# A hybrid S5/HGRN2 decoder block: the first ScalarE reader of each loaded tile tied into program order, and loads, squares, GELU and GLU operands in stages

## The chip, the cores and the metric

The kernel runs on one core of a Trainium2 chip. The metric is device microseconds of one execution, the median of several runs; a profiled execution of the same program gives the trace.

## The reference

x is 2048 tokens of 1024 channels, all float32. One block is computed:

```python
xn = rms_norm(x, norm_w)
proj = xn @ w_in            # 1024 x 5632
u_a, z_a, q_b, f_b, i_b, og_b, z_b, g_a, g_b = split(proj)
y_a = s5_branch(u_a, z_a, ...)    # 32 groups, 64-dim complex diagonal scan, GELU, GLU, * silu(z_a)
y_b = hgrn2_branch(q_b, f_b, i_b, og_b, z_b, ...)   # 4 heads of 128, chunked gated recurrence
merged = sigmoid(g_a) * (y_a @ w_proj_a) + sigmoid(g_b) * (y_b @ w_proj_b)
return rms_norm(x + merged @ w_out, final_norm_w)
```

## The kernel before

**Precision.** A float32 operand of a large product is split into two float32r parts: ScalarE copies it (`hi`), VectorE subtracts (`lo`). This is `split` (L118 to L120), so nearly every such copy has line L119 and every subtraction L120. Each product is three matmuls (hi*hi, hi*lo, lo*hi).

**Stages.** The tokens are two halves, a = 0 and 1. The input projection is done per slice of 256 columns by a seven-product Strassen scheme (`strassen`, L425 on): per product p there are twelve 128x512 matmuls, and PSUM is copied out by L464 (`u`, `s`, ScalarE) and L467 (VectorE). d0 and d1 are the projections of the two halves. Between their products, and in the tail after d1, other work is laid in by hand: HGRN2 (`hgrn_core`, `hgrn_fin`), the state-space branch (`ssm_build`, then `ssm_batch` for eight batches per half), `gelu`, the GLU (`glu_prep` prepares its operands, `glu` multiplies), `merge`, and the output projection (`out_w` loads and splits its weights, `out_proj` multiplies).

**Order.** TensorE's order is written out: `timed` (L1372) steps a generator of dense work, one step of mostly twelve matmuls at a time, and ahead of step t runs the events due at t. An event steps another generator to its next `yield`. The other engines' queues are filled by the framework's scheduler: it goes by program order as priority, but issues an instruction earlier when it takes its inputs to be there, by its own estimate of when loads land. Each queue is then executed in order, so an instruction whose tile has not landed holds everything behind it. All loads and most stores are issued on SP's queue; `u_evac`, `gate_evac` and `ssm_batch` store through ScalarE's.

**Tiles.** Pools have few buffers: `y` tiles (128x1024) two, `wr` tiles (128x1024) three, `wo` five, `s` five, `e` two, `r` (128x512) 56. A tile of a pool is given out again when its last reader is through; a load into it waits for that on SP's queue.

**What the change touches.** `norm_stats` (L178) squares x of one quarter for the RMS norm; for a = 1 it is called at steps 2 and 8 of d0's run with HGRN2, each time four loads into `y` tiles and four squares with accumulation (L189 to L191). `x_load` (L285) reloads transformed x (`xq`, in a `y` tile) and splits it (`X1..h`). `stage_w` and `split_w` (L306 to L320) load and split a projection weight. `w_ops` (L370) loads a raw input weight (`rw`, `get`, L381) and forms the seven Strassen operands; for a = 0 these are stored to DRAM (`wc`, L391) and for a = 1 reloaded (L375). `ssm_batch` (L748) loads W/U and V/M (each pair one tile: WU from `y` or `wr`, VM from `wr` or `wo`), builds or reloads cos/sin (CC, SS; `csv` stores them for the other half, L782), then does the products `psg` (L791), the rotation and scan, and `psy` (L829), whose result goes to `y_d`. `gelu` (L837) reloads `y_d` into a `y` tile `yy`, copies it reordered into the `wr` tile `ya` (L844), and needs a square, two VectorE operations, a sigmoid and a product before `ya` is stored (L851). `glu_prep` (L1171) loads `ya` in pairs into `y` tiles (`gy`) and z (`gz`), splits (`gh`, `gl`) and multiplies z. `glu` (L1188) takes one step per output tile: matmuls, sigmoid `gs`, product, split into `yh`, `yl`.

## Time and profile before

| | us |
|---|---|
| median of three runs | 1539.39 (1536.45 to 1541.62) |
| the profiled execution | 1540.05 |
| its span, first to last instruction | 1538.3 |
| TensorE busy in it | 1467.0 |
| VectorE busy | 1100.8 |
| ScalarE busy | 637.6 |
| TensorE's mean granted clock | 0.984 of full speed |

Busy time counts an instruction's own time, waits of the next instruction on the same engine are its idle time, and the trace names what ended each such wait. PE is TensorE, DVE VectorE, ACT ScalarE, SP the queue of SyncE. A line name can be a helper's (L119 is every ScalarE split), so tiles tell groups apart. Times of the rows below are microseconds from the span's start unless marked ns.

### The profile page before, as it was taken

The numbers are of one execution on the slowest core, as the hardware profiler recorded it, in microseconds if no ns is written. First come the engines' busy times: TensorE is split into PE (matmuls) and PEld (weight loads), VectorE is DVE, ScalarE is ACT, GpSimd is POOL, SyncE is SP. The second block draws the span as 40 slices with busy tenths as digits, with TensorE's granted clock in tenths as the row PEclk, the third lists the DMA queues.
The fourth block names the chain that finished last, engine by engine and source line by source line (L and its number), as shares of the span: only waits on it lengthen the run. The fifth ranks groups of instructions, "written<-read, shape, count | busy, mean of one in ns | idle before, by whom it ended". The sixth has DMA issues, their size and how long they took to land.

```text
span 1538.3 us, 21386 instructions
## 1 busy us (share of the span) xinstructions
PE 1467.0 (95%) x7360; PEld 1207.3 (78%) x7360; DVE 1100.8 (72%) x2409; ACT 637.6 (41%) x1391; POOL 3.6 (0%) x24
## 2 busy tenths in 40 slices
PE   7997999999999999999989999999989899899997
PEld 5776788788888777878878887788878688688886
DVE  5798688678678659956665887776649877765445
ACT  7456454454454634323323455333353332532222
POOL 0000000000000000000000000000000000000000
PEclk9998999999999999999999999999999999999999
DMA  9539778977977883786668559677977854854602
GB/s 336 175 115 305 284 278 295 316 255 269 331 264 286 285 271 119 186 245 197 231 201 313 174 163 294 217 259 264 327 236 234 266 184 137 274 171 131 212 14 103
DMA packets 192060, 354.53 MB, mean 230 GB/s; under 512 B 65680, under 2 KB 74896, under 8 KB 191952
## 3 DMA queue, kind: packets, MB, share of 16 engines
q1 hardware_dynamic: 163792, 328.00, 63.6%
q10 hardware_dynamic: 28160, 25.17, 4.8%
q8 instruction: 58, 0.95, 0.3%
q14 instruction: 50, 0.41, 0.1%
HBM read 214.17 MB, written 138.94 MB: 230 GB/s over the span
## 4 chain that ended last, share of the span: by engine, by line
PE 68%; DVE 15%; DMA 10%; ACT 3%; issue 3%; SPq 0%; ACTq 0%; DVEq 0%
PE pd L458 14%; PE pd L460 13%; PE pd L459 13%; PE pf L1284 3%; PE pf L1285 3%; PE pf L1286 3%; PE pp L1112 2%; PE pp L1111 2%; PE pp L1110 2%; PE sc L979 2%; DMA y_d<-T 1%; DVE w L120 1%; DMA xb<-in_xt_dram 1%; DMA xq<-xo_d 1%; PE pd L355 1%
## 5 line engine op out<-in xcount | busy, mean ns | idle before, releaser
L119 ACT ACTIVATE w<-rw 128x512 fp32r<-128x512 f32 x110 | 68.7, 628 | 112.7 <-PE pd L460 67.9
L1284 PE MATMUL pf<-ho,mh 128*128 128x512 f32 x256 | 101.2, 395 | 5.2 <-ACT mh L119 5.2
L1286 PE MATMUL pf<-ho,ml 128*128 128x512 f32 x256 | 100.6, 393 | 0.5 <-DVE ml L120 0.5
L1285 PE MATMUL pf<-lo,mh 128*128 128x512 f32 x256 | 100.3, 392 | 0.0
L464 ACT ACTIVATE u<-pd 128x512 f32<-128x512 f32 x80 | 47.5, 594 | 106.0 <-PE pd L460 103.3
L120 DVE TENSOR_TENSOR w<-rw,w 128x512 fp32r<-128x512 f32 x110 | 75.3, 685 | 16.9 <-ACT w L119 16.6
L467 DVE TENSOR_TENSOR u<-u,pd 128x512 f32<-128x512 f32 x80 | 54.8, 685 | 33.5 <-PE pd L460 22.8
L355 PE MATMUL pd<-xh,hw 128*128 128x512 f32 x128 | 52.4, 409 | 9.0 <-ACT hw L119 6.7
L1284 PEld LDWEIGHTS pf<-ho,mh 128*128 128x128 f32 x256 | 48.6, 190 | 15.4 <-ACT mh L119 5.5
L1286 PEld LDWEIGHTS pf<-ho,ml 128*128 128x128 f32 x256 | 48.4, 189 | 11.6 <-DVE ml L120 1.6
L1285 PEld LDWEIGHTS pf<-lo,mh 128*128 128x128 f32 x256 | 48.6, 190 | 9.9
L119 ACT ACTIVATE mh<-sgl 128x512 fp32r<-128x512 f32 x32 | 20.0, 629 | 86.7 <-DVE sgl L1227 86.3
L356 PE MATMUL pd<-xl,hw 128*128 128x512 f32 x128 | 51.2, 400 | 0.0
L357 PE MATMUL pd<-xh,lw 128*128 128x512 f32 x128 | 50.9, 397 | 0.0
L980 DVE COPY_PREDICATED s_buf<-masks,sc 128x256 f32<-128x256 uint8 x64 | 32.5, 508 | 25.0 <-PE sc L979 25.0
L1110 PE MATMUL pp<-yh,hpa 128*128 128x512 f32 x128 | 50.2, 392 | 0.0
L1112 PE MATMUL pp<-yh,lpa 128*128 128x512 f32 x128 | 49.9, 390 | 0.2 <-DVE lpa L120 0.2
L1111 PE MATMUL pp<-yl,hpa 128*128 128x512 f32 x128 | 50.0, 390 | 0.0
L1226 DVE TENSOR_TENSOR sgl<-sgl,pp 128x512 f32<-128x512 f32 x48 | 32.7, 683 | 23.0 <-PE pp L1112 22.9
L1016 DVE TENSOR_TENSOR Q<-Q,t 128x256 f32<-128x256 f32 x96 | 40.5, 422 | 10.0 <-PE sc L991 9.9
L974 ACT ACTIVATE KX<-K 128x128 f32<-128x128 f32 x128 | 32.6, 304 | 35.6 <-DVE K L1017 26.3
L979 PEld LDWEIGHTS sc<-Q,KX 128*128 128x128 f32 x256 | 38.0, 189 | 8.9 <-issue 1.8
(915 smaller groups left out, 4431.6 us busy)
## 6 DMA issues: line engine op xcount, KB each, us to landing
wc<-w SPq DMA_DIRECT2D x126, 512.0 KB, 3.4
w<-wc SPq DMA_DIRECT2D x126, 512.0 KB, 4.6
rw<-in_wi_dram SPq DMA_DIRECT2D x44, 512.0 KB, 4.6
sgl<-sg_d SPq DMA_DIRECT2D x48, 256.0 KB, 3.2
sg_d<-u ACTq DMA_DIRECT2D x32, 256.0 KB, 3.5
ro<-in_wo_dram SPq DMA_DIRECT2D x16, 512.0 KB, 5.1
hh<-in_xn_dram SPq DMA_DIRECT2D x32, 256.0 KB, 5.1
out_dram<-hh SPq DMA_DIRECT2D x32, 256.0 KB, 2.4
```

The lines of the kernel that those rows point to most:

```text
L119: S.activation(hi, raw, AF.Copy)
L120: V.tensor_tensor(lo, raw, hi.bitcast(F32), op=ALU.subtract)
L458: mm(o, w[:, 0, k], xh, start=(first and k == 0), stop=False, skip_group_check=True)
L459: mm(o, w[:, 0, k], xl, start=False, stop=False, skip_group_check=True)
L460: mm(o, w[:, 1, k], xh, start=False, stop=(k == 3), skip_group_check=True)
L979: mm(ps[:, :, c, :], ch(kx, c), qp, start=True, stop=True)
L1110: mm(ps, hi[:, k, fs], yh, start=(k == 0), stop=False)
L1111: mm(ps, hi[:, k, fs], yl, start=False, stop=False)
L1112: mm(ps, lo[:, k, fs], yh, start=False, stop=(k == last))
L1284: mm(o, mh[:, ts_], hi, start=(kk == 0), stop=False)
L1285: mm(o, mh[:, ts_], lo, start=False, stop=False)
L1286: mm(o, ml[:, ts_], hi, start=False, stop=(kk == 7))
```

## The change

`pin(ins)` ties an instruction behind the one that the program has just before it on the same engine, so that the scheduler can't issue it earlier; it adds an order, not a wait for a result. `split` gets `hold`, which pins its ScalarE copy; it is set where the copied tile was just loaded: `x_load`, `split_w`, `yb_load`, `glu_w`, `glu_prep`, `out_w`. `norm_stats` keeps only a = 0; for a = 1 `norm_stats1` loads two tiles ahead and squares over ten steps, pinned. `gelu` becomes five stages with the first of its four copies pinned; `glu_prep` loads both pairs in two steps and splits in four more; `glu_w` and `out_w` yield between load and split; `ssm_batch` loads E first, then W/U, then V/M, and stores cos/sin after the rotation; the steps of the events are moved to match. In half 1, raw weights of `SL_QF` come from `wr` instead of `y` tiles. `hgrn_block` loads `cin` at level 6 instead of at its start, and `narrow` looks up its weights when it uses them.

```diff
-    def split(raw, hi, lo):
-        S.activation(hi, raw, AF.Copy)
+    def pin(ins):
+        return tc.keep_in_program_order(ins)
+
+    def split(raw, hi, lo, hold=False):
+        i = S.activation(hi, raw, AF.Copy)
+        if hold:
+            pin(i)
         V.tensor_tensor(lo, raw, hi.bitcast(F32), op=ALU.subtract)
...
+    def norm_stats1():
+        tiles = {}
+        for i in range(10):
+            if i >= 2:
+                xr = tiles.pop(i - 2)
+                pin(S.activation(xr, xr, AF.Square, accum_out=ssx[:, 6 + i : 7 + i]))
+            if i < 8:
+                tiles[i] = y4(f"xr1{i}")
+                nc.sync.dma_start(tiles[i], xn[HALF + i * 128 : HALF + i * 128 + 128, :])
+            yield
...
             pair = r2(f"X1{k}{p}h"), r2(f"X1{k}{p}l")
-            split(raw[:, i * 512 : i * 512 + 512], *pair)
+            split(raw[:, i * 512 : i * 512 + 512], *pair, hold=True)
             X[1][p][k] = pair
...
         i = at[0]
-        split(raw[:, i : i + n], res[0][:, i : i + n], res[1][:, i : i + n])
+        split(raw[:, i : i + n], res[0][:, i : i + n], res[1][:, i : i + n], hold=True)
         at[0] = i + n
...
         def get(kh):
-            raw = (y4 if a and sl != SL_VO else wr4)(f"rw{n}_{kh}").rearrange("p (k n) -> p k n", k=4)
+            raw = (y4 if a and sl < SL_QF else wr4)(f"rw{n}_{kh}").rearrange("p (k n) -> p k n", k=4)
             nc.sync.dma_start(raw, wi[sl, kh])
...
         flat = lambda t: t.rearrange("p g a b -> p g (a b)")
-        WU = wu_pool(f"WU{a}{b}").rearrange("p (i g n) -> p i g n", i=2, g=4)
-        VM = vm_pool(f"VM{a}{b}").rearrange("p (i g n) -> p i g n", i=2, g=4)
-        Wt, U = WU[:, 0], WU[:, 1]
-        Vt, Mt = VM[:, 0], VM[:, 1]
-        nc.sync.dma_start(Wt, w_d[:, gs, :])
-        nc.sync.dma_start(U, u_d[a][b // 2][:, :, g0 : g0 + 4, :].rearrange("s p g c -> (s p) g c"))
-        nc.sync.dma_start(Vt, v_d[:, gs, :])
-        nc.sync.dma_start(Mt, m_d[:, gs, :])
-        CC, SS = t4("CC"), t4("SS")
         csv = lambda i: cs_d[b][:, i].rearrange("p (g a b) -> p g a b", g=4, a=8)
-        T = t4("T")
         if a == 0:
             nc.sync.dma_start(E[:, :, 32:48], eh_d[:, gs, :])
+            yield
+        CC, SS = t4("CC"), t4("SS")
+        T = t4("T")
+        if a == 0:
             lr_ = E[:, :, 0:16].unsqueeze(2).to_broadcast(sh)
             hi_ = E[:, :, 40:48].unsqueeze(3).to_broadcast(sh)
-            yield
             V.tensor_tensor(CC, lr_, hr_, op=ALU.mult)
             V.tensor_tensor(SS, lr_, hi_, op=ALU.mult)
-            yield
-            V.tensor_tensor(T, li_, hr_, op=ALU.mult)
-            V.tensor_tensor(SS, SS, T, op=ALU.add)
-            nc.sync.dma_start(csv(0), CC)
-            nc.sync.dma_start(csv(1), SS)
         else:
             nc.sync.dma_start(SS, csv(1))
+        WU = wu_pool(f"WU{a}{b}").rearrange("p (i g n) -> p i g n", i=2, g=4)
+        Wt, U = WU[:, 0], WU[:, 1]
+        nc.sync.dma_start(Wt, w_d[:, gs, :])
+        nc.sync.dma_start(U, u_d[a][b // 2][:, :, g0 : g0 + 4, :].rearrange("s p g c -> (s p) g c"))
+        yield
+        if a == 0:
+            V.tensor_tensor(T, li_, hr_, op=ALU.mult)
+            V.tensor_tensor(SS, SS, T, op=ALU.add)
+        VM = vm_pool(f"VM{a}{b}").rearrange("p (i g n) -> p i g n", i=2, g=4)
+        Vt, Mt = VM[:, 0], VM[:, 1]
+        nc.sync.dma_start(Vt, v_d[:, gs, :])
+        nc.sync.dma_start(Mt, m_d[:, gs, :])
         C2, S2 = flat(CC), flat(SS)
...
         V.tensor_tensor(t2[64:128], ps[0:64], S2[0:64], op=ALU.mult)
+        if a == 0:
+            nc.sync.dma_start(csv(0), CC)
+            nc.sync.dma_start(csv(1), SS)
         yield
...
     def gelu(a, i):
-        ya = wr4(f"ya{a}{i}")
         yy = y4(f"yy{a}{i}").rearrange("p (t c) -> p t c", t=8)
         nc.sync.dma_start(yy, y_d[a][i].rearrange("t p g c -> (p g) t c"))
+        yield
+        ya = wr4(f"ya{a}{i}")
         for i4 in range(4):
             dst = ya[:, c0 : c0 + 256] if i4 % 2 == 0 else ya[:, c0 + 255 : (c0 - 1 if c0 else None) : -1]
-            S.activation(dst.rearrange("p (c t) -> p t c", t=8), yy[:, :, i4 * 32 : i4 * 32 + 32], AF.Copy)
+            cp = S.activation(dst.rearrange("p (c t) -> p t c", t=8), yy[:, :, i4 * 32 : i4 * 32 + 32], AF.Copy)
+            if i4 == 0:
+                pin(cp)
         q = yy.rearrange("p t c -> p (t c)")
         S.activation(q, ya, AF.Square)
+        yield
         V.tensor_scalar(q, q, 0.044715, 1.0, op0=ALU.mult, op1=ALU.add)
         V.tensor_tensor(q, q, ya, op=ALU.mult)
+        yield
         S.activation(q, q, AF.Sigmoid, scale=GE)
+        yield
         V.tensor_tensor(ya, ya, q, op=ALU.mult)
...
             elif lv <= 7:
+                if lv == 6 and a == 1 and b == 0:
+                    cin = e2("ci" + n)[:, 0:128]
+                    nc.sync.dma_start(cin, carry_d[h])
                 ps = psc.tile([128, 4, 128], F32, name=f"sc{n}_{lv}", tag="psc")
...
             nc.sync.dma_start(raw, wg[i])
+            yield
             for ft in range(2):
                 lo = r2(f"gwl{i}{ft}").rearrange("p (k n) -> p k n", k=4)
-                split(raw[:, :, ft * 128 : ft * 128 + 128], hi, lo)
+                split(raw[:, :, ft * 128 : ft * 128 + 128], hi, lo, hold=True)
                 glw[i * 2 + ft] = (hi, lo)
...
         G_, zs = gp[a, b] = [], []
+        rs = []
         for k in range(4):
...
             nc.sync.dma_start(z, ft_d["za", a, k][:, bs])
+            rs.append(r)
+            zs.append(z)
+            if k % 2:
+                yield
+        for k in range(4):
             gh, gl = r2(f"gh{a}{b}{k}"), r2(f"gl{a}{b}{k}")
-            split(r, gh, gl)
-            V.tensor_tensor(z, z, r, op=ALU.mult)
+            split(rs[k], gh, gl, hold=True)
+            V.tensor_tensor(zs[k], zs[k], rs[k], op=ALU.mult)
             G_.append((gh, gl))
-            zs.append(z)
             yield
...
             nc.sync.dma_start(raw, wo[nh, kp])
+            yield
             res = ow[a, nh, kp] = []
                 lo = pool.tile([128, 512], F32R, name=f"lo{a}{nh}{kp}{k}", tag="r")
-                split(raw[:, k], hi, lo)
+                split(raw[:, k], hi, lo, hold=True)
                 res.append((hi, lo))
...
         def stats(b):
-            norm_stats(1, b)
+            c0 = 8 + b * 4
+            newton_rsqrt(ssx[:, c0 : c0 + 4], 4, 1.0 / D, rst[:, c0 : c0 + 4])
             dg1[b] = norm_diag(1, b)
         ev = heads(0, 3, 35, 18)
-        ev += [(2, lambda: stats(0)), (8, lambda: stats(1)), (13, lambda: bcast(0)), (18, lambda: bcast(1))]
+        steps(ev, norm_stats1(), [1, 2, 4, 5, 7, 8, 10, 11, 13, 14])
+        ev += [(9, lambda: stats(0)), (12, lambda: bcast(0)), (15, lambda: stats(1)), (18, lambda: bcast(1))]
         xg = chain(*[xprep(1, k, rb1) for k in range(4)])
...
             t = 62 + 9 * i
-            for d in ((-5, -4, -3, -2) if i < 8 else (-3,)) + (0, 1, 2, 3, 6):
+            for d in ((-7, -4, -3, -2) if i < 8 else (-4, -2)) + (0, 1, 2, 3, 6):
                 ev.append((t + d, lambda g=g: step(g)))
             if i % 2:
-                ev.append(((101, 106, 118, 136, 151)[i // 2], lambda i=i: gelu(i // 8, i // 2 % 4)))
-        steps(ev, glu_prep(0, 0), [146, 147, 148, 149])
-        steps(ev, glu_w(), [150, 151, 152, 153])
+                t = (98, 105, 116, 134, 150)[i // 2]
+                steps(ev, gelu(i // 8, i // 2 % 4), [t, t + 3, t + 4, t + 5, t + 6])
+        steps(ev, glu_prep(0, 0), [144, 145, 147, 148, 149, 150])
+        steps(ev, glu_w(), [147, 150, 151, 151, 153, 153])
         timed(d1, 154, ev)
         ev = []
-        steps(ev, glu_prep(0, 1), [0, 1, 2, 3])
+        steps(ev, glu_prep(0, 1), [0, 1, 2, 3, 3, 4])
         for i in range(6):
             g = ssm_batch(1, i + 2, y4, wr4 if i < 2 else wo4f, (psm, "psm"))
-            t = 6 + i * 7
-            for d in (-3, 0, 1, 2, 3, 6):
+            t = 4 + i * 7
+            for d in (-4, -2, 0, 1, 2, 3, 6):
                 ev.append((t + d, lambda g=g: step(g)))
             if i % 2:
-                ev.append((t + 7, lambda i=i: gelu(1, i // 2 + 1)))
-        steps(ev, out_w(0, 0, range(4), rp), [14 + s for s in range(8)])
-        steps(ev, out_w(0, 1, range(4), rp), [28 + s for s in range(8)])
-        steps(ev, glu_prep(1, 0), [51, 52, 53, 54])
+                steps(ev, gelu(1, i // 2 + 1), [t + 7, t + 10, t + 11, t + 11, t + 12])
+        for kp in range(4):
+            steps(ev, out_w(0, 0, (kp,), rp), [12 + 2 * kp, 15 + 2 * kp, 16 + 2 * kp])
+            steps(ev, out_w(0, 1, (kp,), rp), ([24, 27, 28], [26, 29, 30], [36, 40, 40], [37, 41, 41])[kp])
+        steps(ev, glu_prep(1, 0), [52, 53, 54, 55, 55, 55])
 
...
         ev = []
-        steps(ev, glu_prep(1, 1), [0, 1, 2, 3])
+        steps(ev, glu_prep(1, 1), [0, 1, 2, 3, 3, 4])
         for i in range(8):
         steps(ev, out_w(1, 0, (0,), None), [21])
-        steps(ev, out_w(1, 1, (2, 3), rp), [26, 27, 28, 29])
+        for kp in (2, 3):
+            steps(ev, out_w(1, 1, (kp,), rp), [19 + 2 * kp, 22 + 2 * kp, 23 + 2 * kp])
         steps(ev, out_w(1, 1, (0, 1), None), [37, 38])
```

## Rows read from the trace of the kernel before

**Rows 1.** The page: busy us, share, count; then groups (busy us, mean ns, idle before).

```profile
PE 1467.0 (95%) x7360; PEld 1207.3 (78%) x7360; DVE 1100.8 (72%) x2409; ACT 637.6 (41%) x1391; POOL 3.6 (0%) x24
...
L119 ACT ACTIVATE w<-rw 128x512 fp32r<-128x512 f32 x110 | 68.7, 628 | 112.7 <-PE pd L460 67.9
...
L120 DVE TENSOR_TENSOR w<-rw,w 128x512 fp32r<-128x512 f32 x110 | 75.3, 685 | 16.9 <-ACT w L119 16.6
```

**Rows 2.** Waits of TensorE: who, for whom, us in total, times, longest us.

```profile
PE pd L458 <- ACT u L464: 13.4, 4, 6.6
...
PE pg L1110 <- ACT gh L119: 6.7, 2, 3.9
PE py L1081 <- ACT ys L1077: 5.7, 3, 2.3
PE pf L1284 <- ACT mh L119: 5.2, 1, 5.2
PE pd L458 <- DMA w<-wc: 4.5, 2, 2.6
```

**Rows 3.** Waits of ScalarE, the two groups for GELU and the squares.

```profile
ACT ya L844 <- DMA yy<-y_d: 22.5, 6, 6.7
...
ACT xr L191 <- DMA xr<-in_xn_dram: 10.3, 5, 3.0
```

**Rows 4.** Timeline of ScalarE at 129 us: start, us, instruction, idle before.

```profile
129.23 1.06 ACT L191 ACTIVATE xr<-xr 128x1024 f32<-128x1024 f32 x1 [2.61 <-DMA xr<-in_xn_dram]
...
130.69 0.57 ACT L464 ACTIVATE u<-pd 128x512 f32<-128x512 f32 x1
```

**Rows 5.** Timeline of ScalarE at 1131 us, around GELU of the second half.

```profile
1130.90 2.09 ACT L844 ACTIVATE ya<-yy 128x256 f32<-128x256 f32 x4 [6.73 <-DMA yy<-y_d]
...
1133.98 0.58 ACT L464 ACTIVATE u<-pd 128x512 f32<-128x512 f32 x1
```

**Rows 6.** Timeline of TensorE, the matmul that waits for that copy.

```profile
1134.61 0.79 PE L458 MATMUL pd<-X105h,w 128*128 128x512 f32 x1 [5.64 <-ACT u L464]
```

**Rows 7.** Timeline of ScalarE at 540 us, a split of reloaded x.

```profile
539.79 0.63 ACT L119 ACTIVATE X122h<-xq 128x512 fp32r<-128x512 f32 x1 [3.50 <-DMA xq<-xo_d]
```

**Rows 8.** Timeline of SP's DMA issues at 800 us.

```profile
799.65 0.34 SPq L782 DMA_DIRECT2D cs_d<-CC  x1
...
800.56 0.40 SPq L375 DMA_DIRECT2D w<-wc  x1
```

**Rows 9.** Windows at lower clock: us, busy PE PEld DVE ACT POOL, granted clock, DMA.

```profile
...
128.60:135.43 6.83, 4.11 (x10) 3.25 (x11) 2.85 (x17) 3.19 (x7) 0.00 (x0) 0.50 0.98 364
541.61:545.02 3.41, 3.41 (x10) 2.70 (x10) 2.17 (x4) 3.29 (x8) 0.00 (x0) 0.50 0.30 101
...
1132.12:1138.95 6.83, 4.34 (x10) 3.46 (x11) 5.02 (x7) 4.61 (x7) 0.00 (x0) 0.50 0.43 168
1224.28:1234.52 10.24, 8.27 (x26) 6.58 (x27) 9.27 (x19) 3.80 (x8) 0.00 (x0) 0.50 0.84 267
...
sum 44.36, PE 36.88 PEld 29.35 DVE 31.99 ACT 20.80 POOL 0.10; mean PE 4.10 PEld 3.26 DVE 3.55 ACT 2.31 POOL 0.01
```

**Rows 10.** Window of the merge before 1214 us, same columns.

```profile
1165.00:1214.00 49.00, 48.78 (x239) 40.75 (x238) 44.02 (x77) 16.22 (x28) 0.00 (x0) 1.00 0.76 248
```

**Rows 11.** Timeline of TensorE, first and last matmul of one Strassen step.

```profile
1126.09 0.39 PE L458 MATMUL pd<-X104h,w 128*128 128x512 f32 x1
...
1128.59 0.39 PE L460 MATMUL pd<-X134h,w 128*128 128x512 f32 x1
```

**Rows 12.** Timeline of SP's DMA issues, start of the tail.

```profile
1138.90 0.32 SPq L851 DMA_DIRECT2D ya_d<-ya  x1
...
1148.56 0.33 SPq L758 DMA_DIRECT2D WU<-w_d  x1
```

**Rows 13.** Landing times of the loads of `gy` (view of one tile).

```profile
DMA to landing us min/median/max: 2.9/4.9/5.7
```

**Rows 14.** Landing times of the loads of `WU` (view of one tile).

```profile
DMA to landing us min/median/max: 2.7/5.2/7.6
```

More of the change, by code (lines that the diff above doesn't have):

```diff
@@ L939, in hgrn_block @@
         Sb = s_buf[b]
-        if a == 1 and b == 0:
-            cin = e2("ci" + n)[:, 0:128]
-            nc.sync.dma_start(cin, carry_d[h])
         KX = h2("KX" + n, "x")
@@ L1096, in yb_pair @@
             pair = r2(n + "h"), r2(n + "l")
-        split(y, *pair)
+        split(y, *pair, hold=hold)
         YB[a, h, b] = pair
@@ L1340, in wide, with narrow @@
                         yield
-        def narrow(nh, w):
+        def narrow(nh):
             for tt in range(8):
@@ L1348, in narrow @@
                 for kp in range(4):
-                    products(nh, kp, tt, o, w[kp])
+                    products(nh, kp, tt, o, ow[a, nh, kp])
                     if kp == 1:
@@ L1357, in out_proj @@
         if a == 0:
-            yield from narrow(0, [ow[a, 0, kp] for kp in range(4)])
+            yield from narrow(0)
         else:
             yield from wide(0, {})
-        yield from narrow(1, [ow[a, 1, kp] for kp in range(4)])
+        yield from narrow(1)
     def run(*gens):
```

20 lines of the change are left out of this document (7 added, 13 removed).

## Prediction

> **What bounds the kernel now.** I read the page first. TensorE is busy 95% of the span and ScalarE 41% [rows 1], so the kernel can only get faster where TensorE stands still or runs at its lower clock. Next, TensorE's waits [rows 2]: the long ones name ScalarE instructions, L464 (the PSUM copy that a Strassen product needs before TensorE may go on) with 13.4 us, the GLU operands `gh` with 6.7, the normalised heads `ys` with 5.7, the merged gate `mh` with 5.2, and, without ScalarE, the cached weights `w<-wc` with 4.5. An engine that is busy 41% is not late because it has too much to do, so I read what it waited for itself. Two of its groups wait for transfers, 22.5 us for GELU's `yy` and 10.3 us for the squares' `xr` [rows 3]. The timelines show how that reaches TensorE. At 125 us the square of an `xr` that has not landed holds ScalarE for 2.61 us, and the `u` copy that stands behind it in the queue starts at 130.69 [rows 4]; TensorE is idle 6.6 us there, the longest of the four waits of L464. At 1124 us ScalarE stands 6.73 us in front of GELU's first copy, then runs the copies and a square, and `u` starts at 1133.98 [rows 5]; TensorE idles 5.64 us for it [rows 6]. A reader of a loaded tile that stands too early in ScalarE's queue holds what is queued behind it. The windows at the lower clock come last: the granted clock is 0.50, the lower of its two levels (1.2 of 2.4 GHz), for 44.36 us in nine stretches, each after one of these stops, and TensorE is busy for 36.88 us of them [rows 9]. I count half of the busy time in such a stretch as lost, as its matmuls run at the lower of the two levels.
>
> **The squares.** Eight 128x1024 loads and squares stay, 1.06 us each [rows 4]; they go to ten steps with a lead of two tiles, and are pinned. What stood behind them was the `u` copy. Recovered: 6.6 us, and half of the 4.11 us at the lower clock behind it [rows 9], 8.65 us. Between a load and its square lie at least two steps of twelve matmuls; a step takes 2.73 us, since 11 of them start within 2.50 us [rows 11].
>
> **GELU.** Load, copies, arithmetic and store become five stages over five steps, and the first copy is pinned three steps behind the load. Around 1129 us that gives back 5.64 us plus half of 4.34 [rows 9], 7.8 us. The two other waits of L464 make up the rest of its 13.4 us [rows 2], 1.2 us. Up to here 17.6 us.
>
> **The splits of reloaded x.** `X122h` holds ScalarE for 3.50 us right ahead of `ys` [rows 7], whose longest wait is 2.3 us [rows 2], and 3.41 us at the lower clock follow [rows 9]: 2.3 + 1.7 = 4.0 us.
>
> **State-space batches.** E is loaded two steps earlier, W/U and V/M later, and the two stores of cos/sin go behind the rotation by CC and SS. SP's queue is moved with them: the store of CC is issued at 799.65 and the reload `w<-wc` that TensorE waits for only behind it, at 800.56 [rows 8]. I count the shorter of the two `w<-wc` waits (4.5 - 2.6 = 1.9 us, [rows 2]) and one stretch of 3.41 us at the lower clock, of which [rows 9] shows the pattern (five of the nine are alike): 3.6 us. The other wait I count at nothing; it could go too (2.6 us).
>
> **Weights and the merge.** The output weights' loads and splits are spread out and pinned. At 1220 us `mh` is 5.2 us late [rows 2] and 8.27 busy microseconds run at the lower clock [rows 9], 9.3 us together. But here VectorE is nearly the bound: busy 44.02 of the 49 us before [rows 10], so at most its 5.0 idle microseconds can come back. Bounds 0 and 9.3; I take 6.0, the 5.0 plus 1.0 for a shorter stretch at the lower clock.
>
> **GLU operands.** Loads go one or two steps ahead of the splits. `gh` costs 6.7 us in two waits [rows 2] and two stretches of 3.41 us follow, 3.4 us: together 10.1. One rest stays: the split of k=3 is now pinned behind the previous step's `yh`, that is behind a sigmoid, a product and a split (0.63 to 0.69 us each, [rows 1], 2.0 us after the step), and its own low part is ready 1.3 us later, at 3.3; TensorE wants it after ten matmuls, at 2.27. One microsecond at each of two places: 8.1 us come back.
>
> **What the change adds.** All pinned splits queue behind a ScalarE instruction that may wait for TensorE; behind a pinned one stand the sigmoids and `mh` splits, and VectorE's low parts wait for it. The exposed place is the pool of two `y` tiles. In the trace GELU's tile is released at about 1138.9 (store of `ya`), the second pair of GLU operands takes it at once, and the next W/U waits until 1148.56 [rows 12]. After the change W/U is asked for at step 0, ahead of the second pair (step 1). It takes GELU's tile, and the pair must wait for the first pair's splits, which are pinned to steps 2 and 3. With T the start of the second GLU half: the split of k=1 ends at T - 2.73 + 2.0 + 0.63 = T - 0.1, its low part and product 1.4 later, the load lands 4.9 us (median, [rows 13]) after that, the split ends at T + 6.8, and TensorE wants it after six matmuls, at T + 1.4. A new stop of 5.4 us, and as the stops of 5.6 and 6.6 us carried 2.1 at the lower clock, 7.4 us. Bounds: 0, if the pair gets GELU's tile after all, and 9.5, if the lower clock lasts as it did at 1224 us (4.1). I take 7.4.
>
> Also, W/U of two later batches meets GELU's tile in the same pool. It is freed by a batch's last products and wanted one step later: landing takes 5.2 us (median, [rows 14]) against 2.73, 2.5 us each, 5.0 us. Bounds 0 and 2 x (5.2 + 2.1) = 14.6; I stay near the lower end, as the medians do. E's and `cin`'s shorter lives, the weights `rw` moved from `y` to `wr` tiles and the square's sum without its add have no TensorE wait of their own and go at nothing; if `wr` ran short instead, a weight would be late by its own landing, some 5 us.
>
> **The sum.** Recovered 17.6 + 4.0 + 3.6 + 6.0 + 8.1 = 39.3 us, added 7.4 + 5.0 = 12.4 us, net 26.9. The profiled execution takes 1540.05 us (span 1538.3), 0.7 us above the median of the runs, 1539.39: 1540.05 - 26.9 = 1513.1, so 1513 us.
>
> The trace shows TensorE idle in part of the stretches at the lower clock: in the seven that I charge (37.5 us) it is busy 30.4 us [rows 9], and I halve those, 15.2 us. The Trainium skill (TensorE: Matmul & The Clock Gate, Terms) counts a throttled time whole times one minus the clock's ratio, 18.8 us. By that the recovered sum would be at most 3.6 us larger and the time 1509.5; the idle part is already in my waits, so I keep the busy time.
>
> **The rivals.** (1) Everything comes back and the `y` pool hurts nobody: 17.6 + 4.0 + 3.6 + 9.3 + 10.1 = 44.6 us, 1495 us. For it: each of the places charged has a transfer's wait of ScalarE or SP ahead of it. Against it: VectorE at 90% in the merge [rows 10].
>
> (2) Only the two early places come true: squares and GELU 17.6 and x 4.0, while merge, GLU and cos/sin stay as they are and the 12.4 us of new stops come: 1531 us. For it: the pins order ScalarE alone; SP and VectorE are still ordered by the scheduler.
>
> (3) The pins don't do what they say: only the first of GELU's four copies is tied, and if the other three are issued as early as now, ScalarE waits in front of them instead; what the squares bring, the `y` pool takes: within 0.3% of 1539.
>
> (4) Slower, by one mechanism: the two `y` tiles run short all through the tail. Six W/U, two GLU halves, eight places, each a landing and a lower clock, 5.2 + 2.0 = 7.2 us: 57.6 added against 39.3 recovered, 1558 us. It decides from 4.9 us per place (39.3 / 8). For it: W/U is asked for one step earlier in its batch and held ten steps with a batch every seven, while GELU's tile is held five. Against it: W/U is issued 9.7 us after GELU's store today [rows 12], and none of TensorE's long waits is for it [rows 2]. The Trainium skill (Perfetto Trace Analysis, Identifying Performance Opportunities) says that a gap that repeats on the engine that should be saturated can mean there is no room for the next tile; that would be this rival, and then order alone would bring nothing. Today's gaps don't repeat with the batches, so the trace bears it out little.
>
> **How the numbers follow.** Forecast 0.36 (1504 to 1522), rival 1 0.24, rival 2 0.15, rival 3 0.12, rival 4 0.13. Faster by more than 0.3% (4.6 us, about what a measurement of this kernel can tell from no change): 0.36 + 0.24 + 0.15 = 0.75; within it 0.12; slower 0.13. The range runs from just under rival 1, 1493, to the unchanged kernel, 1540, and leaves out rival 4 and a few hundredths below.
>
> **What would show it.** In the changed profile ScalarE's waits for `xr` and `yy` should be nearly gone, TensorE's wait for L464 under 2 us, and the stretches at the lower clock at 130 and 1132 us missing. A wait of TensorE for `gh` of about 5 us at the start of the second GLU half, with W/U issued ahead of the second pair, would show the new stop; waits for `WU` at `psg` the second one. The prediction is wrong if the ScalarE waits go and the idle time of TensorE stays, or if the waits for `yy` stay under another line.

## The result, and the profile after

The changed kernel takes 1555.67 us (median of four runs, 1553.9 to 1558.07) against 1538.97 us for the kernel before (four runs beside it): 1.0104 times as long, 95% interval 1.0087 to 1.0121. It is slower by 16.7 us where 26 us less was forecast. The profiled execution took 1553.9 us with a span of 1552.1, 13.8 us longer than the span before.

The page of the changed kernel, its busy time and two of its groups (columns as in [rows 1]):

```profile
PE 1473.4 (95%) x7360; PEld 1205.8 (78%) x7360; DVE 1102.9 (71%) x2409; ACT 639.2 (41%) x1391; POOL 3.6 (0%) x24
...
L122 ACT ACTIVATE mh<-sgl 128x512 fp32r<-128x512 f32 x32 | 20.2, 630 | 103.2 <-DVE sgl L1252 103.2
L1129 PE MATMUL pp<-yh,hpa 128*128 128x512 f32 x128 | 52.3, 409 | 9.3 <-ACT hpa L122 9.3
```

VectorE and ScalarE have about 2 us more work each. Of the 13.8 us TensorE stands idle for 7.4 more; the other 6.4 are more busy time on the same 7360 matmuls. TensorE's waits in the changed kernel, to be read against [rows 2]:

```profile
PE pp L1129 <- ACT hpa L122: 9.3, 5, 2.8
PE py L1100 <- ACT ys L1096: 8.2, 4, 4.5
...
PE pd L468 <- ACT u L474: 4.8, 1, 4.8
PE pg L1130 <- DVE gl L125: 4.6, 7, 1.6
...
PE pd L468 <- DMA w<-wc: 4.0, 3, 3.3
PE pg L1129 <- ACT gh L122: 3.9, 3, 2.0
PE psg L801 <- DMA WU<-u_d: 2.9, 1, 2.9
```

The waits for `u` fell from 13.4 to 4.8 us and those for `gh` from 6.7 to 3.9, and the 5.2 us for `mh` are gone. At the head stands a wait that the kernel before did not have: `pp`, the product of the merge, for `hpa`, the high part of a projection weight. Where the time went is read from TensorE's timeline, from the first matmul of one stage to the first of the next (us). `pd` are the products of the projections, `pb` those of merge b, the HGRN2 part of the merge:

| stretch | before | after | difference |
|---|---|---|---|
| start to the 601st `pd` matmul (squares at 130) | 179.3 | 170.4 | -8.9 |
| to merge b (`pb`) | 354.9 | 353.0 | -1.9 |
| to the 2001st `pd` (reloaded x) | 74.8 | 74.1 | -0.7 |
| to the 3001st `pd` (batches, cos/sin) | 298.5 | 301.2 | +2.7 |
| to the first GLU (`pg`; GELU at 1130) | 234.7 | 239.5 | +4.8 |
| first GLU, to the merge (`pp`) | 22.7 | 30.5 | +7.8 |
| merge, to the output projection (`pf`) | 49.6 | 68.8 | **+19.2** |
| output projection, to the second GLU | 108.4 | 103.4 | -5.0 |
| second GLU to the last matmul | 207.6 | 203.4 | -4.2 |

One profile of each kernel stands behind this table. The kernel of run e8 below is that of before up to the tail, and its first five stretches are 178.3, 356.7, 76.3, 299.5 and 234.5 us, up to 1.8 us off the column of before; differences of about 2 us are therefore not told apart from chance.

So the kernel is 10.8 us ahead where merge b starts, still 4.0 ahead at the first GLU, and 23 behind after the merge. The windows of the tail, before and then after (columns as in [rows 9]), show what the merge is short of:

```profile
1142.20:1164.90 22.70, 22.70 (x106) 18.93 (x105) 18.57 (x30) 14.05 (x23) 0.00 (x0) 1.00 0.64 221
1164.90:1214.50 49.60, 49.38 (x242) 41.24 (x241) 44.12 (x78) 16.69 (x29) 0.00 (x0) 1.00 0.76 249
1214.50:1322.90 108.40, 101.81 (x474) 84.78 (x473) 82.66 (x193) 39.53 (x74) 0.00 (x0) 0.95 0.58 197
```

```profile
1168.70:1237.50 68.80, 58.45 (x256) 45.55 (x255) 56.37 (x97) 23.87 (x40) 0.00 (x0) 0.90 0.78 258
1237.50:1340.90 103.40, 98.17 (x459) 80.89 (x457) 68.16 (x168) 32.31 (x64) 0.00 (x0) 0.98 0.50 174
```

Before, the merge had TensorE idle for 0.2 us and VectorE busy 89%. After, TensorE is idle 10.4 us (68.80 - 58.45) and its clock falls to 0.90, and VectorE, the engine that I thought bound it, is busy only 82%. No engine is full; they wait for each other in a ring. VectorE, ScalarE and TensorE at 1186 us in the changed kernel:

```profile
1183.62 0.69 DVE L1251 TENSOR_TENSOR sgl<-sgl,pp 128x512 f32<-128x512 f32 x1
1184.22 0.68 DVE L810 TENSOR_TENSOR T<-T,T 128x512 f32<-128x512 f32 x1
1184.82 0.69 DVE L1252 TENSOR_TENSOR sgl<-sgl,sgl 128x512 f32<-128x512 f32 x1
```

```profile
1185.54 0.63 ACT L122 ACTIVATE mh<-sgl 128x512 fp32r<-128x512 f32 x1 [4.12 <-DVE sgl L1252]
1186.08 0.61 ACT L122 ACTIVATE hpa<-rpa 128x512 fp32r<-128x512 f32 x1
```

```profile
1186.74 0.68 PE L1129 MATMUL pp<-yh,hpa 128*128 128x512 f32 x1 [2.62 <-ACT hpa L122]
```

`mh` splits a gated sum (`sgl`) that VectorE has to finish first (L1251, L1252, with an operation of a batch, L810, between them); VectorE needs TensorE's last product `pp` for it; the tied `hpa` stands behind `mh`; and TensorE needs `hpa` for its next product. In the kernel before ScalarE ran the same copies long ahead, here the first five:

```profile
1148.43 1.05 ACT L119 ACTIVATE hpa<-rpa 128x1024 fp32r<-128x1024 f32 x1
1149.90 0.62 ACT L119 ACTIVATE hpa<-rpa 128x512 fp32r<-128x512 f32 x1
1151.67 0.62 ACT L119 ACTIVATE hpa<-rpa 128x512 fp32r<-128x512 f32 x1
...
1158.15 0.61 ACT L119 ACTIVATE hpa<-rpa 128x512 fp32r<-128x512 f32 x1
1159.31 0.62 ACT L119 ACTIVATE hpa<-rpa 128x512 fp32r<-128x512 f32 x1
```

The Trainium skill (PSUM — Partial Sum Buffer, Engine vs sequencer instructions) calls the queues of ScalarE and VectorE strict FIFO; the two ScalarE rows at 1185 us agree, `hpa` starting 0.54 us after `mh` and not in the 4.12 us ahead of it.

My theory was therefore: the pin on `split_w` costs the merge its 19 us. The rivals: the steps to which the batches, GELU and the output weights were moved do it; or a transfer that comes late. (No copy of `rpa` waits for its load in the changed kernel, so it is not a late `rpa` that TensorE's waits for `hpa` come from.)

### The profile page after: what moved, and what is told of

It is laid out like the page before. It is cut to its first block, busy times and chain, and to the rows that moved or that the text cites. A ratio compares the mean times of both kernels' runs of the same rounds, so it can differ in the third digit from the quotient of the medians.

```text
span 1552.1 us, 21370 instructions
## 1 busy us (share of the span) xinstructions
PE 1473.4 (95%) x7360; PEld 1205.8 (78%) x7360; DVE 1102.9 (71%) x2409; ACT 639.2 (41%) x1391; POOL 3.6 (0%) x24
## 4 chain that ended last, share of the span: by engine, by line
PE 70%; DVE 16%; DMA 9%; issue 2%; ACT 2%; SPq 1%; ACTq 0%; DVEq 0%
PE pd L468 13%; PE pd L470 13%; PE pd L469 13%; PE pf L1311 4%; PE pf L1312 4%; PE pf L1310 4%; PE pp L1131 3%; PE pp L1129 2%; PE pp L1130 2%; PE sc L995 1%; DMA gz<-za_d 1%; DMA xq<-xo_d 1%; DMA rw<-in_wi_dram 1%; DMA xb<-in_xt_dram 1%; PE psy L842 1%
## 5 line engine op out<-in xcount | busy, mean ns | idle before, releaser
L122 ACT ACTIVATE w<-rw 128x512 fp32r<-128x512 f32 x110 | 68.5, 628 | 103.4 <-PE pd L470 63.1
L474 ACT ACTIVATE u<-pd 128x512 f32<-128x512 f32 x80 | 47.7, 596 | 101.0 <-PE pd L470 97.2
L477 DVE TENSOR_TENSOR u<-u,pd 128x512 f32<-128x512 f32 x80 | 54.8, 685 | 44.3 <-PE pd L470 30.2
L1251 DVE TENSOR_TENSOR sgl<-sgl,pp 128x512 f32<-128x512 f32 x48 | 32.9, 685 | 26.9 <-PE pp L1131 23.7
L1318 ACT ACTIVATE pf<-hh 128x512 f32<-128x512 f32 x32 | 19.4, 605 | 70.6 <-DVE hh L1316 70.5
```

What stands on the lines that cost most here:

```text
L122: i = S.activation(hi, raw, AF.Copy)
L477: V.tensor_tensor(z[key], z[key], ps, op=ALU.add)
```

## The experiments

Lengths are those of the table above; a ratio is to the kernel before, run on the same chip beside each.

### One pin back, four copies tied, the squares alone, no pins

```diff
 x1: -  split(raw[:, i : i + n], ..., hold=True)      # split_w
     +  split(raw[:, i : i + n], ...)
 x2: -  if i4 == 0: pin(cp)                           # gelu
     +  pin(cp)
 x4: before + norm_stats1() at its steps, nothing else
 x5: -  return tc.keep_in_program_order(ins)          # pin
     +  return ins
```

> The changed kernel with one pin taken back: the split of staged projection weights (split_w; the high parts hpa, hpb) is no longer tied to program order; all the rest of the change stays. Theory A: the merge of half 0 (first pp to first pf) grew from 49.6 to 68.8 us because the tied hpa copy stands right behind the mh split, which waits for VectorE's gate. Untied, hpa runs early again: the merge is back at about 50 us, TensorE's waits for hpa (9.3 us in 5) and three of the four low-clock stretches between 1186 and 1245 us go, and the time is 1555.7 - 19 = 1536.5 us (1533 to 1540), the early gain of 9 to 11 us unchanged. Rival B: the merge is late because the output weights are loaded and split in it at other steps and with pins of their own, and VectorE (90% busy before) serves them ahead of the gates; then hpa is only the neighbour that comes last, the merge stays above 62 us and the time above 1549 us.

Measured: 1.0088 (1.0055 to 1.0122), not distinguishable from the changed kernel. The merge did lose 6.0 us (62.8), but the GLU starts 1.1 us later, the output projection takes 2.7 us more and the last stretch 3.3. The wait for `hpa` is gone, and the low part takes its place:

```profile
1219.17 0.80 PE L1131 MATMUL pp<-yh,lpa 128*128 128x512 f32 x1 [7.14 <-DVE lpa L125]
```

VectorE had stood 3.29 us ahead of it for a reload of `sgl`:

```profile
1214.52 0.69 DVE L1251 TENSOR_TENSOR sgl<-sgl,pp 128x512 f32<-128x512 f32 x1 [3.29 <-DMA sgl<-sg_d]
```

SP issued that reload at 1209.10 us, behind GELU's load of `yy` (1208.62), and had stood 6.5 us ahead of `yy` for the store of `y_d` that it reads. So the late transfer is part of this run's longest stop. Rival B's numbers hold (merge above 62 us, time above 1549), but run e6 below speaks against its mechanism, the output weights. Theory A misses the time: the pin is not the only cause.

> The changed kernel with all four copies of GELU tied to program order instead of the first alone. Theory A: TensorE's stop of 4.83 us at 1125 us stays in the changed kernel because three untied copies of yy run ahead of the tied one and wait for the load. With all four tied that stop and the low-clock stretch of 6.83 us behind it go: 1555.7 - 7 = 1548.7 us (1546 to 1552), ScalarE's wait for yy falls from 19.0 us to below 5. Rival B: the load of yy itself is late (its tile comes free late), three steps are no lead, and a tied first copy waits as long where it stands: within 2 us of the changed kernel, 1554 to 1558 us. Rival C: another stage takes up the gain: the GLU starts 5 us earlier, but its second half then waits longer for the tiles that batch and GELU hold, and the end moves by less than 2 us.

Measured: 1.0104 (1.0071 to 1.0138), nothing gained. The wait for `u` L474 is gone, as A says; a wait of 2.35 us for VectorE's `u` L477 is left in its place, and the GLU starts at 1137.9 instead of 1138.2. Rival C is nearest, with the loss ahead of the GLU already: the waits for `ys` grew from 8.2 to 10.3 us.

> The kernel before with one part of the change alone: the squares of the second half in ten steps, loads two tiles ahead, each square tied to program order. Theory A: this is the whole of the gain that the changed kernel shows at 180 us (8.9 us), and it keeps to the end, since TensorE is the bound: 1539.0 - 8.7 = 1530 us (1528 to 1532). Rival B: the gain is eaten by a later wait for a transfer that starts at its own time (cached weights at 790 us, GELU's store at 1130 us); then the first product of the merge b part starts 9 us earlier but the end comes less than 4 us earlier, 1535 us or more.

Measured: 0.9940 (0.9916 to 0.9963), 8.5 us below the kernel before by the medians. The 601st `pd` comes at 171.2, the tail has its old lengths (GLU 22.7, merge 49.9), and the lead in between stays at 5 to 8 us. Theory A.

> The changed kernel without any pin: the stages, the moved steps and the moved stores stay, and the scheduler may issue every copy and square as early as it takes its tile to be there. Theory A: the merge loses its 19 us as in the run without the weights' pin, but the squares of the second half and the copies of reloaded x run too early again and hold the PSUM copies; about 1555.7 - 19 + 5 = 1541 us (1536 to 1547), with a stop of TensorE behind L474 near 130 us again. Rival B: the stages alone put each reader far enough behind its load, so that the early gain stays without pins: 1533 to 1538 us.

Measured: 1.0072 (1.0048 to 1.0096). Merge 62.7 us without any pin, the squares' gain kept (170.9), and the stop for `u` at 1129 us is 7.3 us. At 1553.0 us it misses both ranges. Stages alone fix the squares, as rival B says; without a pin the readers of the last loads ahead of the GLU still run early; and the merge is long without any pin.

### The tail's steps

```diff
 e5: -  t = 4 + i * 7;  d in (-4, -2, 0, 1, 2, 3, 6);  gelu at t+7, t+10, ... t+12
     +  t = 6 + i * 7;  d in (-3, -3, 0, 1, 2, 3, 6);  gelu all at t+7
     +  out_w: load and first split in one step, 14 + 2 kp and 28 + 2 kp
 e6: the out_w lines of e5 alone
 e7: e5, and no pin in split_w and out_w, all four copies of gelu tied
 e8: before, with  t = 4 + i * 7  for the batches (gelu at t + 9, its old step)
 e11: before, with  pin  on split_w's copy
```

> The changed kernel with the events of the first tail (GLU, merge and output projection of half 0) put back to their steps of before: batches 2 to 7 of half 1 at 6 + 7i with W/U asked for three steps ahead, GELU's five stages all in one step seven later, output weights loaded and split in the same step. All pins stay. The run without the weights' pin showed that the pin is not the cause: the merge was 6 us shorter, but the end came at the same time, with TensorE waiting for VectorE's low part of a weight whose load had been issued late. Theory A: the tail is bound by VectorE (busy 48 of 50 us in the merge before), and the change moved a batch's rotation and a GELU (some 8 us of VectorE work) from the output projection, where there is room, into the GLU and the merge, and made the three wr tiles be held for longer. With the old steps the stretch from the first GLU matmul to the last merge matmul falls from 99 us to near the 72 us of before, and the time is 1555.7 - 17 = 1539 us (1533 to 1543). Rival B: it is the pins and the order of the loads within a batch (cos/sin ahead of W/U, V/M last), which stay here: the stretch stays above 90 us and the time above 1550 us.

> The changed kernel with only the output weights back at their old steps (load and first split in one step, second split one later, 14 to 21 and 28 to 35). Theory A (the batches' and GELU's VectorE work is what fills the merge): little changes, 1552 to 1557 us, the merge stays above 62 us. Rival B (the three wr tiles: each output weight keeps its tile three steps longer, so the next projection weight rpa is asked for late): rpa is issued earlier, the merge falls to 55 us or less and the time to 1540 to 1547 us.

> A version for the better: the run with the tail at its old steps, and besides no pin on the projection and output weights and all four copies of GELU tied. Left of the change are the squares, the tied copies of reloaded x, the stages of GELU and of the GLU operands in the first part, and the batches' order. Theory A: early gain 9 to 11 us kept, GELU's stop at 1125 us gone (7 us), second GLU half still stopped: 1539 - 9 - 5 = 1525 us (1520 to 1532), faster than before and than the squares alone (1532). Rival B: what stays of the change in the tail (second pair of GLU operands behind W/U, GLU weights and GELU's arithmetic two steps later) costs as much as is gained: 1533 to 1540 us.

> The kernel before with one part of the change alone: the batches of the first tail two steps earlier (4 + 7i instead of 6 + 7i), GELU and all else at their old steps, no pins. Theory A (VectorE work moved into a stretch that VectorE bounds): the stretch from the first GLU matmul to the last merge matmul grows by about 5 us of moved rotation or more, the output projection gives back 2 us or less; 1541 to 1549 us. Rival B (the batch's steps don't matter, the pins or the held tiles do): 1536 to 1541 us.

> The kernel before with one part of the change alone: the high-part copies of staged projection weights (split_w) tied to program order, all steps as before. Theory A: the pin alone does to the merge what the batches' steps alone do: hpa stands behind an mh copy that waits for VectorE, the merge of half 0 grows from 50 to about 63 us, as in the run with the tail at its old steps and the pins on, and the output projection gives back some 5 to 7 us; 1545 to 1551 us at a kernel before of 1540, that is 5 to 9 us slower. Rival B: it needs the pins on the output weights too; then merge under 55 us and within 3 us of the kernel before.

Measured, as ratio and length of the merge: e5 1.0027 (1.0007 to 1.0046), 63.0 us; e6 1.0111 (1.0085 to 1.0138), 67.9; e7 0.9995 (0.9977 to 1.0013), 49.4; e8 1.0030 (1.0012 to 1.0048), 67.2; e11 1.0053 (1.0035 to 1.0071), 63.4. Against what was expected: e5 fits neither theory (1546.6 us, GLU and merge together 88.1); the VectorE time of 48 us that it gives for the merge is 44.12 in the windows above. e6 is theory A, one microsecond above its range: the output weights' steps are not the cause. e7 gains nothing, as rival B says (1542.4 us, with the kernel before at 1542.9 beside it). e8 lies in theory A's range, but GLU and merge grew by 18.1 us where 5 or more were expected, and the output projection gave back 13.1 where 2 were. e11 is theory A, with 10.0 us given back instead of 5 to 7. Together with the first four runs they fill a square:

| merge, us | projection weights free | tied |
|---|---|---|
| tail at its old steps | 49.6 (before), 49.4 (e7) | 63.4 (e11), 63.0 (e5) |
| batches two steps earlier | 67.2 (e8), 62.8 (x1), 62.7 (x5) | 68.8 (after), 67.9 (e6) |

Each of the two causes alone lengthens the merge by 13 to 18 us, and both together by 18 to 19: where the engines already wait for each other, the second cause adds only 2 to 6 us. (Kernels in one cell differ in other parts, and by up to 4.5 us.) All pins together (e5) cost the merge no more than that of `split_w` alone (e11). Taking back the pin alone (x1) left the end where it was. Taking back the tail's steps alone (e5) made the end 0.8% earlier: the merge is 5.9 us shorter than after the change and the first GLU 5.4. The windows of the merge in e11, e8 and e7:

```profile
1171.50:1234.90 63.40, 54.32 (x242) 42.10 (x241) 53.36 (x97) 22.13 (x38) 0.00 (x0) 0.95 0.80 265
```

```profile
1168.50:1235.70 67.20, 57.14 (x258) 46.67 (x256) 58.12 (x104) 23.50 (x39) 0.00 (x0) 0.87 0.84 274
```

```profile
1167.20:1216.60 49.40, 49.27 (x242) 41.32 (x240) 43.98 (x78) 16.92 (x30) 0.00 (x0) 1.00 0.77 256
```

e11 has as many matmul records as before (242), so its growth splits: 9.1 us idle (63.40 - 54.32) against 0.2, and 4.9 us more busy time (54.32 against 49.38) at a clock of 0.95. Its ScalarE rows show the same neighbours:

```profile
1200.30 0.63 ACT L119 ACTIVATE mh<-sgl 128x512 fp32r<-128x512 f32 x1 [3.83 <-DVE sgl L1229]
1200.84 0.61 ACT L119 ACTIVATE hpa<-rpa 128x512 fp32r<-128x512 f32 x1
```

The Trainium skill (Perfetto Trace Analysis, Identifying Performance Opportunities) reads a gap that repeats on the engine that should be saturated as a possible lack of room for the next tile. After the change the gap for `hpa` repeats five times in the merge, in e11 four times (6.9 us). e11 has the tiles, steps and loads of the kernel before, and no copy of `rpa` waits for its load in it, so here it is order and not room.

In e8 no pin exists, and the largest stop comes through another reader of a loaded tile: ScalarE stands in front of GELU's copies, `mh` behind them, VectorE's `ml` behind that, and the low part that TensorE wants behind `ml`. ScalarE, VectorE and TensorE of e8:

```profile
1214.61 2.12 ACT L844 ACTIVATE ya<-yy 128x256 f32<-128x256 f32 x4 [5.07 <-DMA yy<-y_d]
...
1217.73 0.61 ACT L119 ACTIVATE mh<-sgl 128x512 fp32r<-128x512 f32 x1
```

```profile
1218.38 0.69 DVE L120 TENSOR_TENSOR ml<-sgl,mh 128x512 fp32r<-128x512 f32 x1 [3.03 <-ACT mh L119]
...
1221.69 0.69 DVE L120 TENSOR_TENSOR lpa<-rpa,hpa 128x512 fp32r<-128x512 f32 x1
```

```profile
1222.43 0.79 PE L1112 MATMUL pp<-yh,lpa 128*128 128x512 f32 x1 [7.17 <-DVE lpa L120]
```

Part of it comes back: VectorE's work that fell into the merge is missing from the output projection, which takes 95.3 us in e8, 98.4 in e11 and 103.4 after the change, against 108.4. e8 and e11 end 4.0 and 7.6 us above the kernel before, by the medians; for e8 that is about what the merge and the output projection leave (17.6 - 13.1), for e11 these leave 3.8, and its profile is also 4.0 us longer ahead of the first GLU, in a stretch where none of TensorE's waits is for a tied copy. How e8's 17.6 us divide between VectorE's moved rotation and this one stop was not separated; as in x1, the stop begins at GELU's `yy`, whose load waits for the store of `y_d`. e7 keeps the early gain of 8.5 us at merge b and the old merge, and still ends where the kernel before does: it loses 5.0 and 3.1 us in the two stretches of d1 and 6.4 in the first GLU.

### Building up from the squares

```diff
 e9:  x4 + gelu cut after its load, all four copies pinned, at [t - 3, t]; last one at [150, 153]
 e10: e9 + hold=True in x_load
 e12: e10 + batches of the tail at 7 + 7 i, GELU with them
 e13: e9 + the changed glu_prep, at [146, 146, 147, 148, 149, 150], [0, 1, 1, 2, 3, 3], ...
 e14: after + W/U and V/M of the first tail batch at step 3
```

> The kernel before with the squares in ten tied steps and GELU cut in two: load, three steps later all four copies (tied) and the rest; the last one before the tail loads at step 150 and copies at 153 instead of all at 151. The tail is as before. Theory A: GELU's stop of 5.0 to 5.6 us at 1129 us and the low clock behind it go, the first tail keeps its old length (GLU 23, merge 50 us): 7 us below the squares alone, which stood 8.5 us below the kernel before: 15 us below it (12 to 18). Rival B: as in the run with all four copies tied, TensorE's waits for ys near 970 and 1100 us grow from 3.4 to 9 us because the copies and VectorE's arithmetic for GELU come between those of the heads; then less than 11 us below the kernel before.

Measured: 0.9922 (0.9896 to 0.9948), 11.1 us below the kernel before and, with e10, the best of all: 1528.52 us (1526.44 to 1530.42). Some 2.6 us of it are GELU's, by the 8.5 of x4. That is short of theory A's 12 to 18, and rival B's growth of the `ys` waits is there but smaller (5.1 us instead of 9). TensorE's stop has only changed its owner; ScalarE and TensorE of e9:

```profile
1123.25 0.63 ACT L122 ACTIVATE gh<-gy 128x512 fp32r<-128x512 f32 x1 [4.55 <-DMA gy<-ya_d]
1123.79 0.58 ACT L478 ACTIVATE u<-pd 128x512 f32<-128x512 f32 x1
```

```profile
1124.42 0.80 PE L472 MATMUL pd<-X105h,w 128*128 128x512 f32 x1 [4.72 <-ACT u L478]
```

> The same with the splits of reloaded x tied as well. Theory A: the run with the weights' pin taken back was 3.9 us shorter than the kernel before from the first matmul of merge b to the middle of d1's first products (70.9 against 74.8 us); these tied splits alone give it, so 3.5 us less than the run without them. Rival B: it took the loads of the weights at their new steps as well; less than 1.5 us.

Measured: 0.9933 (0.9911 to 0.9956), not distinguishable from e9. The stretch with the reloaded x is 2.0 us shorter (72.0 against 74.0), between the two expectations, and the next one 2.2 longer; neither is clear of the scatter between profiles.

> The run with squares, GELU and reloaded x, and the batches of the first tail one step later (7 + 7i) instead of earlier. Theory A: two steps earlier lengthened the merge by 17.6 us and gave 13.1 us back in the output projection, because VectorE's work came ahead of the merge's gates; one step later takes about 2.5 us of it out, but the merge is already at TensorE's own rate (48.8 us busy), so only the stop of 5.2 us behind mh at the start of the output projection can shrink: 2 to 6 us less than without it. Rival B: what leaves the merge comes back in the output projection as the wait for W/U or for low parts: within 2 us.

Measured: 0.9980 (0.9963 to 0.9997), 6.3 us above e10; a miss for both theories. The stop for `mh` went, but the merge took 57.5 us instead of 51.5, with `psy` waiting for VectorE and `pp` 3.1 us for `lpa`, and a W/U came 3.4 us late at 1277. Of the three positions tried the old one has the shortest merge; in e12 GELU moved along with the batches.

> The run with squares and GELU (11.1 us below the kernel before), and the GLU operands as the changed kernel has them, both pairs loaded ahead and their four splits tied, at steps close to the old ones; tail, weights, reloaded x and batches as in the kernel before. In the run with squares and GELU alone ScalarE stood 4.55 us in front of a gh copy at 1119 us, and the PSUM copy u behind it let TensorE wait 4.72 us. Theory A: the reader is early there too; tied, that stop goes, and the two gh waits of half 1 (2.5 and 2.7 us) shrink: 7 to 11 us less than that run, 1518 to 1522 us at a kernel before of 1539.6. Rival B: the loads are late, since two y tiles serve GELU and both operand pairs, and what is tied waits in its own place: within 3 us of that run.

Measured: 0.9961 (0.9943 to 0.9978), some 6 us above e9 (0.0039 of 1540). The end misses both theories. Theory A holds at its place: the stop for `u` is gone, 2.1 us for VectorE's `u` remain, and the stretch up to the first GLU is 228.6 us against 235.1 with the squares alone. But the two GLUs lose it: the first takes 27.8 us instead of 23.7, and the waits for `gl` reach 7.7 us, since the tied splits come after the sigmoids of the previous step.

> The changed kernel with W/U and V/M of the first tail batch asked for at step 3 instead of steps 0 and 2, behind the second pair of GLU operands; nothing else. Theory A: W/U no longer takes GELU's y tile ahead of the pair; gy of the second pair is issued by 1145 us instead of 1150, TensorE's waits for gh and gl (4.0 us in the second half) and the low clock there go, and the first GLU falls from 30.5 us to 25 us or less. As the merge is bound by VectorE and ScalarE's order, the end need not move by as much: 1549 to 1556 us. Rival B: GELU's arithmetic (3 us of VectorE moved behind the first GLU matmul) and the pinned splits make the second half late; it stays above 28 us.

Measured: 1.0136 (1.0108 to 1.0163). The pair is loaded first, no wait for `gh` or `gl` is left in the first GLU, and W/U is late instead; SP's queue and TensorE of e14:

```profile
1147.48 0.32 SPq L870 DMA_DIRECT2D ya_d<-ya  x1
1147.89 1.20 SPq L1199 DMA_DIRECT2D gy<-ya_d  x2
...
1154.12 0.32 SPq L787 DMA_DIRECT2D WU<-w_d  x1
```

```profile
1158.00 2.05 PE L801 MATMUL psg<-WU 128*128 128x128 f32 x8 [5.69 <-DMA WU<-u_d]
```

The first GLU still takes 30.6 us. Both theories fall in part: asked for later but wanted as early as after the change, W/U waits in place of the pair. e5 has the same two `y` tiles and also asks for W/U at step 3, behind the pair, but its batch comes two steps later; there no wait for W/U is left and the first GLU takes 25.1 us.

## Why the prediction was wrong, step by step

The sum missed by 40.7 us: 26.9 less was forecast for the profile and 13.8 more measured. 19.2 of them lie in the merge, for which the sum had no term. Nearly as much, 18.9, lies in the last two stretches of d1, where 11.4 less (GELU 7.8, cos/sin 3.6) was forecast and 7.5 more came. A sign that I had named came too: ScalarE still waits 19.0 us in five places for `yy`, against 22.5 in six [rows 3].

**The squares** (8.65 us): right. 8.9 us in the profile after, 8.5 us alone (x4). ScalarE's longest wait for `xr` is 2.3 us and holds no PSUM copy that TensorE wants.

**GELU** (7.8 us): did not come. I wrote that the first copy is pinned and let the stop go; rival 3 had said what happens to the other three. ScalarE in the changed kernel:

```profile
1127.84 1.62 ACT L858 ACTIVATE ya<-yy 128x256 f32<-128x256 f32 x3 [5.97 <-DMA yy<-y_d]
1129.25 0.64 ACT L474 ACTIVATE u<-pd 128x512 f32<-128x512 f32 x1
...
1136.46 0.69 ACT L858 ACTIVATE ya<-yy 128x256 f32<-128x256 f32 x1 [0.40 <-ACT eg L890]
```

Three copies run 8.6 us ahead of the tied one and hold `u`: 4.83 us for TensorE instead of 5.64 [rows 6]. The size was nearly right (with copies and `gh` tied, e13 is 6.5 us shorter there than x4), the step "the first copy is pinned, so the wait goes" was wrong. The 1.2 us for the other `u` waits came.

**Reloaded x** (4.0 us): 0.7 after; 3.9 in x1 and 3.7 in e7, in both of which the weights were free, and 2.0 in e10, given back later.

**Cos/sin** (3.6 us): did not come. The waits for `w<-wc` went from 4.5 to 4.0 us; x4, e8 and e9, which leave these batches alone, have 6.0 to 6.2, so one profile does not show what the move brought. And `py` waits 8.2 us for `ys` instead of 5.7. VectorE of the changed kernel ahead of the wait of 4.5 us at 968 us, where the small rows are the chain of the inverse root that `ys` needs:

```profile
964.90 0.17 DVE L162 TENSOR_SCALAR rso<-smi 128x8 int32<-128x8 int32 x1
964.97 0.69 DVE L864 TENSOR_SCALAR yy<-yy 128x1024 f32<-128x1024 f32 x1
965.58 0.16 DVE L164 TENSOR_TENSOR small<-rso 128x8 f32<-128x8 f32 x1
...
966.34 1.22 DVE L865 TENSOR_TENSOR yy<-yy,ya 128x1024 f32<-128x1024 f32 x1
967.47 0.16 DVE L166 SCALAR_TENSOR_TENSOR rso<-small,rso 128x8 f32<-128x8 f32 x1
...
968.90 1.22 DVE L869 TENSOR_TENSOR ya<-ya,yy 128x1024 f32<-128x1024 f32 x1
970.04 0.15 DVE L166 SCALAR_TENSOR_TENSOR rso<-small,rso 128x8 f32<-128x8 f32 x1
```

GELU's three VectorE operations (3.1 us) now lie between the links of that chain, since its stages were moved from step 106 to steps 105 to 111; I had counted GELU's ScalarE part only. The same chain in other runs shows that its length is what counts: it lasts 6.2 us in the kernel before (974.34 to 980.52) and in x5 (968.41 to 974.60), 8.1 in e9 (965.14 to 973.25) and 8.7 in the changed kernel (963.48 to 972.13), and TensorE waits 2.0, 2.1, 3.8 and 4.5 us for `ys` behind it. In e9 no GELU operation lies in it, but twelve others do instead of nine. This place costs the changed kernel 2.4 us. At 1103 us the chain is 7.5 us long in both kernels, and the wait grew from 1.3 to 3.1; what makes `ys` late there, and the rest of the 2.7 and 4.8 us that d1 lost, stays open.

**Weights and the merge** (6.0 us gained): the stop for `mh` at 1220 us went, and the output projection, in which it lies, is 5.0 us shorter. (My bound of 5.0 us for it was VectorE's idle time in the merge ahead, another stretch; that it fits is luck.) The merge ahead of it had no term in the sum, and this is the step that failed: it grew by 19.2 us, and the tied projection weights alone bring 13.8 of such growth (e11), the batches' two steps alone 17.6 (e8). Under "what the change adds" I wrote that tied splits queue behind an instruction that may wait, named TensorE as what it waits for, and then called the two `y` tiles the exposed place. The tied projection weights got no price, and neither did the batches' two steps, though I had measured VectorE at 90% there. A price of the ties could have been read from the profile of before, in ScalarE's waits in the whole program:

```profile
ACT mh L119 <- DVE sgl L1227: 86.3, 26, 5.0
```

and in the window of the merge alone (1164.9 to 1214.5 us):

```profile
ACT mh L119 <- DVE sgl L1227: 18.6, 9, 3.9
```

An `mh` copy that waits stands 3.3 us on average (86.3 / 26) in front of what is tied behind it, in the merge 2.1 (18.6 / 9). Six `hpa` copies behind it are some 12 us by the merge's own waits and up to 20 by the program's, an estimate from these rows; e11 measured 13.8 in the merge and 7.6 at the end.

**GLU operands** (8.1 us): 2.8 us in the waits for `gh`, while those for `gl` went from 0.6 to 4.6; the second GLU as a whole is 5.0 us shorter (28.4 against 33.4 to its merge). But it takes 30.2 us in e8 and 30.3 in e9, which leave these operands as they were, so 2 us of it at most are clearly the change's.

**The second GLU half** (7.4 us added): the first GLU grew by 7.8, with SP's order as predicted:

```profile
1144.40 0.32 SPq L870 DMA_DIRECT2D ya_d<-ya  x1
1144.81 0.38 SPq L787 DMA_DIRECT2D WU<-w_d  x1
...
1150.19 0.80 SPq L1199 DMA_DIRECT2D gy<-ya_d  x2
```

The stop is smaller than I had worked out, 2.0 us for `gh` and 2.0 for `gl` instead of 5.4, and the stretch at the granted clock of 0.50 behind it costs more (5.80 busy us from 1156.19 on, half of them 2.9, where I took 2.1); that the total fits so well is in part luck. e14 and e5 together show that the order of the loads alone does not decide it: the batch's own step does too. No run had a third `y` tile. **W/U** (two places of 2.5 us): one, of 2.9 us, in the output projection.

Rival 4 gave 1558 us, 2 us from the result, by another way: I let eight places wait for `y` tiles, and two did. Its number is no support for its mechanism; the ring in the merge was in none of the cases.

## What to carry to other kernels

Before a copy is tied into program order, read what the instruction ahead of it waits for: its mean wait in that stage times the number of ties is a rough price, and it can be read from the old profile (2.1 us times six here, 13.8 measured in the stage). In this merge TensorE, ScalarE and VectorE feed each other once per tile, and early issue by the scheduler was the slack; both a tie and two moved steps consumed it. A tie on one reader of a tile can move the stop to the next reader that is free to run early (three copies of `yy` after the change, `gh` in e9), so look at all readers of a load, and then count what the engine behind them must do in the new place.

## What the runs showed that I had not expected

The two causes in the merge don't add: 13.8 and 17.6 us alone, 19.2 together. And the length of a chain of tiny VectorE operations is set by what lies between them: VectorE's timeline of the kernel before has its last three links at 979.95, 980.15 and 980.35 us, 0.20 us apart with nothing between, while three links with other work between took 1.92 us there (977.83 to 979.75) and 2.57 in the changed kernel (967.47 to 970.04).
